# A first MLP product made of seven block products, with weight sums by adding DMAs, and GpSimd without arithmetic

## The chip, the core and the metric

The kernel runs on one core of one Trainium2 chip, in one launch. The metric is the time of one execution on the device in microseconds; shown is the median of several executions. The profile comes from one further execution.

## The reference, cut to what matters

One layer of a decoder, for 512 positions of width 1024, in float32:

```python
h = rms_norm(x, norm_mix)
proj = h @ w_in                      # HGRN2 and attention heads side by side
x = x + mixed @ w_out                # mixed: the heads' outputs
h = rms_norm(x, norm_xattn); mem_n = rms_norm(mem, norm_mem)
x = x + cross_attention(h, mem_n, w_xq, w_xk, w_xv, w_xo)
h = rms_norm(x, norm_mlp)
x = x + square(relu(h @ w_ff1)) @ w_ff2      # w_ff1 1024 x 4096, w_ff2 4096 x 1024
return rms_norm(x, norm_final)
```

`rms_norm` divides each position by the root of its mean square plus 1e-6 and multiplies by a gain.

## The kernel before

**Products.** Activations lie with features on the 128 partitions and positions in columns (T = 512). Each product is computed to nearly float32 accuracy by three matmuls: a weight `wr` is split into `wh` (rounded to fp32r, on ScalarE) and `wl = wr - wh` (VectorE), the activation likewise into `hi` and `lo`, and TensorE adds `wh*hi + wh*lo + wl*hi` in PSUM. A *unit* is a weight tile of 128x1024 (512 KB): one feature block of 128 outputs over all 1024 inputs, 8 blocks x 3 = 24 matmuls. `need(u)`, called ahead of unit u, issues the loads (up to six units ahead, three raw buffers, on SP's queue) and the splits (two units ahead, four buffers) of later units.

**Order.** Up to the output projection's neighbourhood the program is written under `manual_schedule`: each engine executes in the order in which the code emits; a small model (`Pace`) with due times decides in between when pieces of side work (norms, recurrence, attention: the generators) are emitted. From `ordered.__exit__` on (L508), the rest, among it both MLP products, is ordered by the compiler's automatic scheduler. Each engine runs its own instructions in order and waits by semaphores.

**The stages.** The head computes the first units `hf` while x is loaded (`split_x`, `square_x`): xhi on ScalarE, xlo on VectorE; the sum of squares is collected in Sx (GpSimd) and Sy (VectorE); `split_part(..., PO)` gives three lower parts of weights to GpSimd. `nr` is the matmul that sums the squares over partitions with ones, in a high and a low part (`nrh`, `nrl`). During the output projection `wo` the memory's norm is made (`mem_prep`): squares `msq` on ScalarE, folded by GpSimd to Sm, then nr. `hgrn_pre` has two multiplications on GpSimd for each head (ke, eb).

**The MLP.** The first product (tile `f`) has 32 units with 512-wide matmuls; `ev_ff1` takes max(.,0) times the norm's factor on VectorE (`fft`) and squares it on ScalarE into the tiles g. The second product is made of seven block products (Strassen-Winograd): g in four blocks (2 halves of features x 2 halves of positions), w_ff2 in four blocks; seven products of sums of blocks, each 8 units of 24 matmuls of 128x256, into the banks X, Y and Z (`PLAN`). Sums of activation blocks (`op_p6` and so on) are made on VectorE, and `make_op` splits them. Sums of weight blocks (u, four sets of eight) are made early in DRAM: a copy by SP's queue, then a DMA that adds, issued by GpSimd (`block_sums`); one of these transfers is emitted with each load from unit 16 on.

**The end.** `norm_part` and `final_half` normalise each half of the positions; the last half's multiplications (`xgf`) are shared by VectorE and GpSimd, and SP's queue writes the output.

Most engine calls go through a helper, so their line in the profile is L115; the tile's name tells them apart.

Of the kernel before, what the change touches and what calls it, by code (L numbers as in the profile page):

```python
# [15 lines left out]
P = 128  # L16
D = 1024
T = 512
# [14 lines left out]
FF2 = MLP + 32  # L33
# [89 lines left out]
def hybrid_layer(ctx: ExitStack, tc: tile.TileContext, xT, memT, ws, vecs, consts, rots, out):  # L123
# [14 lines left out]
    WBUFS, N8, N2, N2E = 4, 12, 14, 8  # L138
# [4 lines left out]
    def s2(dtype, name):  # L143
        return sp.tile([P, T], dtype, tag="s2", name=name, bufs=N2)

    def e2(dtype, name):
        return ep.tile([P, T], dtype, tag="e2", name=name, bufs=N2E)
# [10 lines left out]
    def mem_view(t):  # L158
# [3 lines left out]
    raws, his, los, late = {}, {}, {}, []  # L162
# [4 lines left out]
    F1 = [ws[MLP + 16 * (n // 8) + n % 8] for n in range(32)]  # L167


    B11, B12, B21, B22 = ([ws[MLP + 16 * (2 * i + c) + 8 + 4 * j + n] for c in range(2) for n in range(4)]  # L170
                          for i in range(2) for j in range(2))
    U1, U2, U3, U4 = ([dram.tile([P, D], F32, name=f"u{b}_{j}") for j in range(8)] for b in range(1, 5))
    sources = [ws[u] for u in range(MLP)] + [F1[j // 2 + 16 * (j % 2)] for j in range(32)]
    sources += B11 + U1 + U2 + B22 + U3 + B21 + U4

    def block_sums():

        for o1, i1, a1, o2, i2, a2 in ((U1, B11, B12, U3, B12, B22), (U2, U1, B22, None, None, None),
                                       (U4, U2, B21, None, None, None)):
            for j in range(8):  # L180
                yield nc.sync.dma_start(o1[j], i1[j])
                if o2:
                    yield nc.sync.dma_start(o2[j], i2[j])
            for j in range(8):
                yield nc.gpsimd.dma_start(o1[j], a1[j], accum_op=ALU.add, max_dma_last_dim=D)  # L185
                if o2:
                    yield nc.gpsimd.dma_start(o2[j], a2[j], accum_op=ALU.add, max_dma_last_dim=D)

    AFTER = mybir.DependencyInfo(mybir.DependencyClass.Sync, mybir.DependencyReason.DATA)
    marks = [None]  # L190

    sums_of_blocks = block_sums()

    def load_unit(parts=((0, D),)):
        u = state["load"]
        if u >= FF2 and u % 4 == 3:
            raws[u] = late[0].tile([P, D], F32, tag="rawl", name=f"wr{u}", bufs=1)
        else:
            raws[u] = wpool.tile([P, D], F32, tag="raw", name=f"wr{u}", bufs=RAWS)
# [3 lines left out]
        if u >= 16:  # L203
            dma = next(sums_of_blocks, None)
            if dma is not None:
                tc.add_manual_dep(dma.ins, marks[-2].ins.name, AFTER)

    def split_part(u, a, b, eng=None):
        A.activation(his[u][:, a:b], raws[u][:, a:b], AF.Copy)
        (eng or V).tensor_sub(los[u][:, a:b], raws[u][:, a:b], his[u][:, a:b].bitcast(F32))  # L210

    def split_begin():
        u = state["split"]
        his[u] = wpool.tile([P, D], F32R, tag="whi", name=f"wh{u}", bufs=WBUFS)
        los[u] = wpool.tile([P, D], F32R, tag="wlo", name=f"wl{u}", bufs=WBUFS)
        state["split"] += 1
        return u
# [5 lines left out]

    def need(u):
        marks.append(last_mm[0])
        want_load, want_split = min(UNITS, u + LOAD_AHEAD + 1), min(UNITS, u + SPLIT_AHEAD + 1)
        while state["split"] < want_split or state["load"] < want_load:
            if state["load"] < want_load and state["load"] - state["split"] < RAWS + (u >= FF2):
                load_unit()
            elif state["split"] < want_split:  # L230
                split_unit()
            else:
                break

# [169 lines left out]
    def square_x(k):  # L404
# [18 lines left out]
    split_part(0, 2 * P, D, PO)  # L423
# [3 lines left out]
    split_part(1, D // 2, D, PO)  # L427
# [4 lines left out]
    for k in range(4, KT):  # L432
        split_x(k)
        square_x(k - 2)
        if k == 6:
            split_unit(PO)
# [94 lines left out]
    def hgrn_pre(h):  # L531
# [6 lines left out]
        eb, enb = e2(F32, f"eb{h}"), e2(F32, f"kt{h}")  # L538
# [89 lines left out]
    def ev_q(h, acc):  # L628
        drain(("pre", h))
        H = head[h]  # L630
        qx = [sp.tile([P, 2, 224], F32, tag="s2", name=f"qx{g}", bufs=N2) for g in range(2)]
# [109 lines left out]
    def mem_prep():  # L741
# [12 lines left out]
        PO.tensor_add(sq[:, :1024], sq[:, :1024], sq[:, 1024:])  # L754
        PO.tensor_add(sq[:, :512], sq[:, :512], sq[:, 512:1024])
        PO.tensor_add(S[:, :M], sq[:, :M], sq[:, M:2 * M])
# [137 lines left out]
    def ev_xq(n, acc):  # L894
        z = s2(F32, f"xq{n}")
        V.scalar_tensor_tensor(z, acc, -float(M) ** -0.5, rb2, op0=ALU.mult, op1=ALU.mult)
        hi, lo = e2(F32R, f"xqh{n}"), e2(F32R, f"xql{n}")
# [23 lines left out]
    def ox_act(k):  # L921
# [3 lines left out]
    x2hi = [s8(F32R, f"x2hi{i}") for i in range(2)]  # L925
    x2lo = [s8(F32R, f"x2lo{i}") for i in range(2)]
    S2 = s2(F32, "S2")
    residual_stage(u, ox_act, "xo", [(2, 4)] + ONE * 6, lambda n: x1[n // 4][:, n % 4, :],
                   x1, G_MLP, x2hi, x2lo, S2)
    u += 8  # L930


    early.close()
    lp = ctx.enter_context(tc.tile_pool(name="late", bufs=1, reuse_waits="tile"))
    late.append(lp)
    rb3 = rb1
    start(norm_later(S2, rb3), "n3")
    x2_act = pair(x2hi, x2lo)
    half = T // 2
    g = [s8(F32, f"g{i}") for i in range(6)] + [lp.tile([P, 4, T], F32, name=f"g{i}") for i in (6, 7)]  # L940
# [5 lines left out]
    def ev_ff1(j, acc):  # L946
        n = j // 2 + 16 * (j % 2)
        if j == 0:
            drain("n3")
        t = s2(F32, "fft")  # L950
        V.scalar_tensor_tensor(t, acc, 0.0, rb3, op0=ALU.max, op1=ALU.mult)
        A.activation(g[n // 4][:, n % 4, :], t, AF.Square)
        if n >= 16 and n % 4 == 3:
            k = n // 4 - 4
            V.tensor_sub(part(k, 1), part(k + 4, 1), part(k, 1))

    fm_stage(u, x2_act, T, ev_ff1, "f1", [(2, 1)] + ONE * 30)
    u += 32
# [4 lines left out]
    def op_p1(k):  # L963
        return part(k, 0)

    def op_p5(k):
        return part(k, 1)

    def op_p6(k):
        V.scalar_tensor_tensor(part(k, 1), part(k, 1), -1.0, part(k, 0), op0=ALU.mult, op1=ALU.subtract)  # L970
        return part(k, 1)

    def op_p3(k):
        V.scalar_tensor_tensor(part(k, 0), part(k, 1), -1.0, part(k + 4, 0), op0=ALU.mult, op1=ALU.subtract)
        return part(k, 0)

    def op_p7(k):
        V.scalar_tensor_tensor(part(k, 1), part(k, 1), -1.0, part(k + 4, 1), op0=ALU.mult, op1=ALU.subtract)
        return part(k, 1)

    def op_p2(k):
        return part(k + 4, 0)

    def op_p4(k):
        return part(k + 4, 1)
# [3 lines left out]
    OPS = (op_p1, op_p5, op_p6, op_p3, op_p7, op_p2, op_p4)  # L989

    def make_op():

        i = op_state[0]
        op_state[0] += 1
        src = OPS[i // 4](i % 4)
        if i == 1:
            pieces = [[s2(F32R, f"op1{x}{y}") for x in range(2)] for y in range(2)]
        else:
            both = (lp.tile([P, 4, T], F32R, name="op0") if i == 0 else s8(F32R, f"op{i}")).rearrange("p a b -> p (a b)")
            pieces = [[both[:, :D], both[:, D:]]]  # L1000
# [31 lines left out]
    xg = {}  # L1032
    squares = [0, 0]

    def norm_part(h, t, n):
# [3 lines left out]
        if t not in xg:  # L1039
            xg[t] = mem_view(s8(F32, f"xgf{t}"))  # L1040
        q = Sf[t] if squares[t] == 0 else s2(F32, f"fsq{f}")
        A.activation(q[:, :half], d, AF.Square)
        A.activation(xg[t][:, f], d, AF.Copy, scale=gain(G_FIN, f))
# [3 lines left out]
        elif squares[t] == KT:  # L1047
            start(final_half(t, Sf[t], q, xg[t]), ("fin", t))

    def final_half(nb, S, q, xg):  # L1050
# [8 lines left out]
        for eng, a, b in ((V, 0, 2), (PO, 2, 4), (V, 4, 7), (PO, 7, 8)):  # L1059
            eng.tensor_mul(xg[:, a:b], xg[:, a:b], r[:, None, :].to_broadcast([P, b - a, half]))  # L1060
            SY.dma_start(out[nb, :, a:b], xg[:, a:b])
# [38 lines left out]
    drain(("fin", 1))  # L1100
    assert u + 56 == UNITS
# [73 lines left out]
```

## Time and profile before

| | us |
|---|---|
| median of 3 executions | 771.53 (771.48 to 773.09) |
| the profiled execution | 771.99 |
| its span in the profile | 770.2 |
| TensorE busy (4120 matmuls) | 746.6 |
| VectorE busy | 481.6 |
| ScalarE busy | 375.1 |
| GpSimd busy | 69.4 |
| first MLP product on TensorE, 768 matmuls | 418.4 to 592.6 |
| second MLP product | to 758 |

The span is what the profile covers, from the first to the last instruction; the execution's own time is 1.8 us longer. PE is TensorE's matmul, PEld its weight load, DVE VectorE, ACT ScalarE, POOL GpSimd, SP the engine that only issues DMAs. In a row of the trace the numbers are start and duration in us, and in brackets at the end the idle time of the engine just before the row and what ended it.

### The profile page before, as it was taken

To read this page: it belongs to the slowest core of one execution; us is meant where nothing else is said; L and a number is where in the kernel's file an instruction comes from. 1 tells how busy PE (TensorE), PEld (TensorE's weight loads), DVE (VectorE), ACT (ScalarE), POOL (GpSimd) and SP (SyncE) were. 2 spreads that over 40 slices of the span, in tenths; PEclk is the share of its full clock that TensorE was granted. 3 is DMA by queue.
4 is the path that set the end of the run, shared out by engine and by line. 5 is a ranking of instruction groups with operands and counts; after the bars stand their busy time and mean duration, and the time that the engine had idled before them with its cause. 6 is when DMAs were issued, how large, how long until landed. Compare 5 with 4: busy or idle time off the path is not lost.

```text
span 770.2 us, 10538 instructions
## 1 busy us (share of the span) xinstructions
PE 746.6 (97%) x4120; PEld 643.5 (84%) x4120; DVE 481.6 (63%) x747; ACT 375.1 (49%) x553; POOL 69.4 (9%) x67
## 2 busy tenths in 40 slices
PE   6999999999998999999999999999999999999993
PEld 4788888777786998888888888888888999999993
DVE  6889644877766655766466334243435898676862
ACT  7574546345755453555344433232325455476653
POOL 5123000000132210021001200000000000000011
PEclk9999999999999999999999999999999999999997
DMA  7413434544799997479668872323232555555531
GB/s 269 137 57 136 137 110 153 175 137 130 174 227 207 207 301 260 124 163 291 189 210 167 193 165 86 110 82 110 83 109 85 168 186 191 177 181 184 186 124 54
DMA packets 44801, 123.82 MB, mean 161 GB/s; under 512 B 4144, under 2 KB 21168, under 8 KB 44112
## 3 DMA queue, kind: packets, MB, share of 16 engines
q1 hardware_dynamic: 27376, 105.92, 40.4%
q0 software_dynamic: 16896, 16.78, 14.6%
q8 instruction: 32, 0.52, 0.3%
q10 hardware_dynamic: 480, 0.45, 0.2%
q14 instruction: 17, 0.14, 0.1%
HBM read 121.04 MB, written 35.65 MB: 203 GB/s over the span
## 4 chain that ended last, share of the span: by engine, by line
PE 88%; DVE 5%; issue 3%; ACT 2%; DMA 1%; POOL 0%; POOLq 0%; SPq 0%; DVEq 0%; ACTq 0%
PE f L115 22%; PE X L115 10%; PE xo L115 7%; PE Y L115 6%; PE mkq L115 6%; PE xq L115 6%; PE wo L115 5%; PE Z L115 3%; PE hq L115 3%; PE hg L115 3%; PE mv L115 3%; PE memv L115 3%; PE memk L115 3%; PE xs L115 1%; PE a L115 1%
## 5 line engine op out<-in xcount | busy, mean ns | idle before, releaser
L115 ACT ACTIVATE wh<-wr 128x1024 fp32r<-128x1024 f32 (+2 forms) x158 | 165.0, 1047 | 264.1 <-issue 113.3
L115 DVE TENSOR_TENSOR wl<-wr,wh 128x1024 fp32r<-128x1024 f32 (+1 forms) x155 | 188.7, 1219 | 57.0 <-ACT wh L115 56.4
L115 PE MATMUL f<-x2lo,wh 128*128 128x512 f32 x256 | 99.6, 389 | 0.0
L115 PE MATMUL f<-x2hi,wh 128*128 128x512 f32 x256 | 99.6, 389 | 0.0
L115 PE MATMUL f<-x2hi,wl 128*128 128x512 f32 x256 | 99.6, 389 | 0.0
L115 PE MATMUL X<-op,wh 128*128 128x256 f32 x512 | 93.6, 284 | 1.5 <-DVE op L115 0.8
L115 DVE SCALAR_TENSOR_TENSOR fft<-f,rb 128x512 f32<-128x512 f32 x32 | 22.0, 691 | 96.1 <-PE f L115 96.1
L115 PEld LDWEIGHTS X<-op,wh 128*128 128x128 f32 x512 | 80.1, 192 | 2.4 <-DVE op L115 1.3
L115 PE MATMUL X<-op,wl 128*128 128x256 f32 x256 | 72.4, 284 | 0.0
L115 PEld LDWEIGHTS f<-x2lo,wh 128*128 128x128 f32 x256 | 48.0, 188 | 10.1
L115 PEld LDWEIGHTS f<-x2hi,wl 128*128 128x128 f32 x256 | 48.1, 188 | 10.0
L115 PEld LDWEIGHTS f<-x2hi,wh 128*128 128x128 f32 x256 | 48.0, 188 | 10.0
L185 POOL DMA_DIRECT2D u<-in_ws_dram x24 | 24.5, 1022 | 316.0 <-DMA mraw<-in_memT_dram 129.4
L115 PEld LDWEIGHTS X<-op,wl 128*128 128x128 f32 x256 | 49.0, 192 | 0.1
L115 PE MATMUL Y<-op,wh 128*128 128x256 f32 x256 | 46.2, 283 | 0.0
L115 PEld LDWEIGHTS Y<-op,wh 128*128 128x128 f32 x256 | 39.9, 192 | 0.0
L115 DVE TENSOR_TENSOR op<-g,op 128x1024 fp32r<-128x1024 f32 (+1 forms) x29 | 34.0, 1183 | 5.1 <-ACT op L115 5.1
L115 PE MATMUL Y<-op,wl 128*128 128x256 f32 x128 | 36.2, 283 | 0.0
L115 POOL TENSOR_TENSOR xgf<-xgf,rb 128x512 f32<-128x512 f32 (+1 forms) x4 | 6.3, 1598 | 311.4 <-PE X L115 294.3
L115 ACT ACT_TABLE_LOAD x25 | 32.1, 1283 | 3.1 <-DVE osl L115 1.5
L115 ACT ACTIVATE op<-g 128x1024 fp32r<-128x1024 f32 (+1 forms) x29 | 29.0, 1019 | 4.2 <-PE X L115 1.5
L115 PE MATMUL mkq<-xhi,wl 128*128 128x512 f32 x64 | 26.6, 416 | 0.0
(268 smaller groups left out, 1625.4 us busy)
## 6 DMA issues: line engine op xcount, KB each, us to landing
wr<-in_ws_dram SPq DMA_DIRECT2D x122, 512.0 KB, 3.8
u<-in_ws_dram POOLq DMA_DIRECT2D x32, 512.0 KB, 6.7
wr<-u SPq DMA_DIRECT2D x32, 512.0 KB, 3.4
u<-in_ws_dram SPq DMA_DIRECT2D x16, 512.0 KB, 3.6
u<-u SPq DMA_DIRECT2D x16, 512.0 KB, 5.3
xraw<-in_xT_dram SPq DMA_DIRECT2D x8, 256.0 KB, 6.1
xr<-in_xT_dram SPq DMA_DIRECT2D x8, 256.0 KB, 6.5
mraw<-in_memT_dram SPq DMA_DIRECT2D x1, 1024.0 KB, 4.8
```

The costliest lines, as they stand in the source:

```text
L115: return f(*args, **kw)
L185: yield nc.gpsimd.dma_start(o1[j], a1[j], accum_op=ALU.add, max_dma_last_dim=D)
```

## The change

1. **The first product** is also made of seven block products. Its 32 units become 8 groups (`f1_group`), each for two output features blocks of each half of the 4096; w_ff1 is cut into E00, E01, E10, E11 (halves of the 1024 inputs x halves of the outputs... of a pair of blocks), so a group needs E00, E11, E10 and the sums B = E00 + E01, c = E11 + E01, A = B + E11, D' = E10 + A. Five raw loads per group go through SP's queue; `f1_load` adds E01 to B and to c by two DMAs of GpSimd's queue that add into SBUF; A and D' are VectorE additions (`f1_add`). Each product takes 2 banks x 4 blocks x 3 matmuls of 128x256; 56 splits of 128x1024 take the place of 32. Sums of the activation blocks (OA, OS, OB) are made in `ev_xo`, whose outputs come in the order 0, 4, 1, 5, 2, 6, 3, 7. The banks are taken out by copies (ScalarE) and additions (VectorE) into t1 and t2.
2. **GpSimd** computes nothing: its lower parts and sums in the head, ke and eb, the memory's squares and the last multiplications are VectorE instructions. It still issues the adding DMAs.
3. **The order**: both MLP products are under `manual_schedule`, so in written order. The ScalarE table with logarithm and exponential is loaded in groups 0 and 4 of the first product. Block sums of w_ff2 are emitted with the loads of units 16 to 67 (52) and in the first groups (12); their adding DMAs move pieces of up to 4096 instead of 1024 elements per descriptor row. The lower parts of weights have three buffers (four before) in the MLP; in the last block product the units come in the order 0, 2, 1, 3; the final norm's products are written into g tiles.

```diff
+    F1_ORDER = [(0, 1, 5, 3, 2, 4, 6)] * 7 + [(0, 1, 3, 2, 4, 5, 6)]
+    def f1_load(j, what):
+        r, c = {"A": (0, 0), "B": (0, 0), "C": (1, 1), "D": (1, 0)}[what.upper()]
+        t = f1raw[what, j] = raw_tile(f"w{what}{j}", what in "AD")
+        nc.sync.dma_start(two(t), E[r][c][j].rearrange("n p c -> p n c"))
+        if what in "Bc":
+            nc.gpsimd.dma_start(two(t), E[0][1][j].rearrange("n p c -> p n c"), accum_op=ALU.add)
+    def f1_add(j, out, x, y):
+        V.tensor_add(f1raw[out, j], f1raw[x, j], f1raw[y, j])
+    def f1_prep(j, s):
+        split_raw(split_begin(), f1raw[("ABCAcDd" if j == 7 else "ABDCAcD")[s], j], 0, D)
+        if s == 1:
+            f1_add(j, "A", "B", "C")
...
+        elif s == 1:
+            f1_load(j + 1, "B")
+        elif s == 3:
+            f1_add(j, "D", "D", "A")
+            f1_load(j + 1, "C")
...
+        if s in (2, 6):
+            more_sums()
...
     def need(u):
+        if MLP <= u + SPLIT_AHEAD < FF2:
+            f1_prep(*divmod(u + SPLIT_AHEAD - MLP, 7))
+            return
...
-    split_part(0, 2 * P, D, PO)
+    split_part(0, 2 * P, D, V)
...
-            S, eng = (Sx, PO) if k < 4 else (Sy, V)
+            S, eng = (Sx, V) if k < 4 else (Sy, V)
...
-        PO.tensor_add(sq[:, :1024], sq[:, :1024], sq[:, 1024:])
+        V.tensor_add(sq[:, :1024], sq[:, :1024], sq[:, 1024:])
...
-    fm_stage(u, x2_act, T, ev_ff1, "f1", [(2, 1)] + ONE * 30)
+    ordered = tc.manual_schedule()
+    ordered.__enter__()
+    for j in range(8):
+        f1_group(j)
+        u += 7
...
+            if p == 3 and j in (0, 4):
+                nc.scalar.preload_act_table_set("natural_log_exp_and_others")
...
+                for k in ks:
+                    a_hi, a_lo = op1(p, k)
+                    c = b * T + k * P
+                    w_hi, w_lo = his[w][:, c:c + P], los[w][:, c:c + P]
+                    mm(acc, w_hi, a_hi, p in (0, 1, 5) and k == 0, False)
+                    mm(acc, w_hi, a_lo, False, False)
+                    mm(acc, w_lo, a_hi, False, k == 3)
...
-        for eng, a, b in ((V, 0, 2), (PO, 2, 4), (V, 4, 7), (PO, 7, 8)):
+        for eng, a, b in ((V, 0, 2), (V, 2, 4), (V, 4, 7), (V, 7, 8)):
```

How the instructions stand on the engines, where the steps of the prediction speak of it. First VectorE in the first MLP product, before: a lower part (wl) for each unit, and one evacuation (fft) of each bank.

```order
L115 TENSOR_TENSOR wl_4555<-wr_4456,wh_4554 128x1024
L115 SCALAR_TENSOR_TENSOR fft<-f_4526,rb_217 128x512
L115 TENSOR_TENSOR wl_4589<-wr_4490,wh_4588 128x1024
L115 SCALAR_TENSOR_TENSOR fft<-f_4560,rb_217 128x512
L115 TENSOR_TENSOR wl_4624<-wr_4524,wh_4623 128x1024
L115 SCALAR_TENSOR_TENSOR fft<-f_4594,rb_217 128x512
```

The same engine now, in the third group (wl of c and D', taking out Y and X into t2, then wl of the next group's A and B, the sum A, and the factors):

```order
L115 TENSOR_TENSOR wl_4452<-wc_4210,wh_4451 128x1024
L115 TENSOR_TENSOR wl_4483<-wD_4241,wh_4482 128x1024
L115 TENSOR_TENSOR t_4399<-t_4399,Y_4385 128x256
L115 TENSOR_TENSOR t_4413<-t_4413,Y_4386 128x256
L115 TENSOR_TENSOR t_4399<-t_4399,X_4340 128x256
L115 TENSOR_TENSOR wl_4518<-wA_4419,wh_4517 128x1024
L115 TENSOR_TENSOR t_4413<-t_4413,X_4341 128x256
L115 TENSOR_TENSOR wl_4548<-wB_4307,wh_4547 128x1024
L115 TENSOR_TENSOR wA_4419<-wB_4307,wC_4383 128x1024
L115 SCALAR_TENSOR_TENSOR t_4399<-t_4399,rb_217 128x512
L115 SCALAR_TENSOR_TENSOR t_4413<-t_4413,rb_217 128x512
```

A lower part of the next group now stands between the two banks' evacuations of product 4, and a sum of weights ahead of the factors.

Second, TensorE in the output projection, before (wo_2053 is its fourth unit; the two nr are the memory's norm):

```order
L115 MATMUL wo_2053<-mixhi_1136,wl_1941 128x512
L115 MATMUL wo_2053<-mixhi_1693,wh_1940 128x512
L115 MATMUL wo_2053<-mixlo_1694,wh_1940 128x512
L115 MATMUL nr<-nrh,ones_r 128x256 [waits PE_49,Activation_49]
L115 MATMUL wo_2053<-mixhi_1693,wl_1941 128x512
L115 MATMUL wo_2053<-mixhi_1693,wh_1940 128x512
L115 MATMUL wo_2053<-mixlo_1694,wh_1940 128x512
L115 MATMUL nr<-nrl,ones_r 128x256 [waits DVE_49]
```

And now:

```order
L115 MATMUL wo_2055<-mixhi_1690,wl_1941 128x512
L115 MATMUL wo_2055<-mixhi_1690,wh_1940 128x512
L115 MATMUL nr<-nrh,ones_r 128x256 [waits PE_49,Activation_49]
L115 MATMUL wo_2055<-mixlo_1691,wh_1940 128x512
L115 MATMUL wo_2055<-mixhi_1690,wl_1941 128x512
L115 MATMUL nr<-nrl,ones_r 128x256 [waits DVE_49]
L115 MATMUL wo_2110<-mixhi_1121,wh_1998 128x512
```

The first nr stood behind 14 matmuls of that unit and now stands behind 22; the second stood behind 17 and now stands behind all 24.

Third, ScalarE at the end of the program, before:

```order
L115 ACTIVATE fsq_6754<-x_1905 128x256
L115 ACTIVATE xgf_6151<-x_1905,vec 128x256
L115 ACT_TABLE_LOAD
L115 ACTIVATE rb_2265<-fs,eps 128x256
L115 ACT_TABLE_LOAD
L115 ACTIVATE rb_2265<-rb_2265 128x256
```

And now:

```order
L115 ACTIVATE fsq_7624<-x_1898 128x256
L115 ACTIVATE g_3836<-x_1898,vec 128x256
L115 ACTIVATE fsq_7653<-x_1898 128x256
L115 ACTIVATE g_3836<-x_1898,vec 128x256
L115 ACTIVATE rb_2265<-fs,eps 128x256
L115 ACTIVATE rb_2265<-rb_2265 128x256
```

The two table loads ahead of the logarithm and the exponential are gone.

More of the change, by code (lines that the diff above doesn't have):

```diff
@@ L32 @@
 MLP = 8 + 8 + 4 + 8 + 4 + 4 + 4 + 4 + 8 + 8 + 8
-FF2 = MLP + 32
+FF2 = MLP + 7 * 8
 UNITS = FF2 + 7 * 8
@@ L159, in mem_view @@
         return t.rearrange("p a b -> p (a b)").rearrange("p (k m) -> p k m", k=KT)
-    raws, his, los, late = {}, {}, {}, []
+    raws, his, los, late, n8 = {}, {}, {}, [], [1]
     state = {"load": 0, "split": 0}
     LOAD_AHEAD, SPLIT_AHEAD, RAWS = 6, 2, 3
[L167 to L187, printed above, removed]
+    def f1_block(i, j):
+        us = [MLP + 16 * (n // 8) + n % 8 for n in range(16 * j, 16 * j + 16, 2)]
+        return [ws[u:u + 2, :, i * T:(i + 1) * T] for u in us]
@@ new lines, in f2_block, with two @@
+    def f2_block(i, j):
+        return [ws[MLP + 16 * (2 * i + c) + 8 + 4 * j + n] for c in range(2) for n in range(4)]
+    def two(ap):
+        return ap.rearrange("p (n c) -> p n c", n=2)
+    E, F = ([[f(i, j) for j in range(2)] for i in range(2)] for f in (f1_block, f2_block))
+    FU = [[dram.tile([P, D], F32, name=f"u{b}_{j}") for j in range(8)] for b in range(4)]
+    XO = (0, 4, 1, 5, 2, 6, 3, 7)
+    sources = [ws[u] for u in range(MLP - 8)] + [ws[MLP - 8 + n] for n in XO] + [None] * (FF2 - MLP)
@@ L189, in hybrid_layer, with more_sums, raw_tile @@
+    transfers = block_sums(F, FU)
+    SUMS_FROM = 16
     AFTER = mybir.DependencyInfo(mybir.DependencyClass.Sync, mybir.DependencyReason.DATA)
     marks = [None]
-    sums_of_blocks = block_sums()
+    def more_sums():
+        dma = next(transfers, None)
+        if dma is not None:
+            tc.add_manual_dep(dma.ins, marks[-2].ins.name, AFTER)
+    def raw_tile(name, in_late):
+        if in_late:
+            return late[0].tile([P, D], F32, tag="rawl", name=name, bufs=2)
+        return wpool.tile([P, D], F32, tag="raw", name=name, bufs=RAWS)
@@ L194, in load_unit @@
     def load_unit(parts=((0, D),)):
         u = state["load"]
[L196 to L199, printed above, removed]
+        raws[u] = raw_tile(f"wr{u}", u >= FF2 and (u - FF2) % 5 in (1, 3))
         for a, b in parts:
@@ L202, in load_unit, with later, split_raw, lower @@
         state["load"] += 1
[L203 to L206, printed above, removed]
+        if SUMS_FROM <= u < MLP:
+            more_sums()
+    held = []
+    def later(f):
+        held[0].append(f) if held else f()
+    def split_raw(u, raw, a, b, eng=None):
+        A.activation(his[u][:, a:b], raw[:, a:b], AF.Copy)
+        def lower(hi=his[u], lo=los[u]):
+            (eng or V).tensor_sub(lo[:, a:b], raw[:, a:b], hi[:, a:b].bitcast(F32))
+        later(lower)
     def split_part(u, a, b, eng=None):
-        A.activation(his[u][:, a:b], raws[u][:, a:b], AF.Copy)
-        (eng or V).tensor_sub(los[u][:, a:b], raws[u][:, a:b], his[u][:, a:b].bitcast(F32))
+        split_raw(u, raws[u], a, b, eng)
     def split_begin():
@@ L233, in need @@
                 break
+        if MLP - 6 <= u < MLP - 2:
+            for what in ("A", "B", "CD", "c")[u - MLP + 6]:
+                f1_load(0, what)
     side = []
@@ L630, in ev_q @@
         H = head[h]
-        qx = [sp.tile([P, 2, 224], F32, tag="s2", name=f"qx{g}", bufs=N2) for g in range(2)]
+        qx = [s2(F32, f"qx{g}", (2, 224)) for g in range(2)]
         rbeb = H["rbeb"].rearrange("p (t c) -> p t c", c=P)
@@ L936, in hybrid_layer, with op1 @@
+    fm_stage(u, ox_act, T, ev_xo, "xo", [(2, 4)] + ONE * 6)
+    u += 8
+    def op1(p, k):
+        if p == 0:
+            return OA[0][:, k, :half], OA[0][:, k, half:]
+        if p < 5:
+            return tuple(x[:, (p - 1) * half:p * half] for x in OS[k])
+        return tuple(x[:, (p - 5) * half:(p - 4) * half] for x in OB[k])
+    lp = late[0]
     rb3 = rb1
     start(norm_later(S2, rb3), "n3")
-    x2_act = pair(x2hi, x2lo)
-    half = T // 2
-    g = [s8(F32, f"g{i}") for i in range(6)] + [lp.tile([P, 4, T], F32, name=f"g{i}") for i in (6, 7)]
+    g = [s8(F32, f"g{i}") for i in range(8)]
@@ L958, in hybrid_layer @@
[L958 to L985, printed above, removed]
+    rest = []
+    def f1_tile(t, op, dst):
+        V.scalar_tensor_tensor(t, t, 0.0, rb3, op0=op, op1=ALU.mult)
+        A.activation(dst, t, AF.Square)
+    def f1_end(n, t):
+        k = n // 4
+        A.activation(g[k][:, n % 4, :], t, AF.Square)
+        if n % 4 == 3:
+            V.tensor_sub(part(k, 1), part(k + 4, 1), part(k, 1))
+    def f1_rest():
+        while rest:
+            rest.pop(0)()
```

247 lines of the change are left out of this document (191 added, 56 removed).

## The prediction

> **What bounds the kernel now.** I read the page first: the span, the busy time of each engine, and the shares of the chain that ended last. Then I read that chain in order of time, and then the two MLP stretches, 418.40 to 593.20 (first product) and 593.20 to 758.00 (second).
>
> ```profile
> span 770.2 us, 10538 instructions
> PE 746.6 (97%) x4120; PEld 643.5 (84%) x4120; DVE 481.6 (63%) x747; ACT 375.1 (49%) x553; POOL 69.4 (9%) x67
> PE 88%; DVE 5%; issue 3%; ACT 2%; DMA 1%; POOL 0%; POOLq 0%; SPq 0%; DVEq 0%; ACTq 0%
> ```
>
> TensorE is busy 97% of the span and holds 88% of the chain. Time can only go where matmuls become fewer or shorter, or in the 770.2 - 746.6 = 23.6 us in which TensorE stands. VectorE has 288.6 us left over, GpSimd computes little. The next rows are the chain (start, duration, engine, tile, count) and then windows (start:end, length, and the busy time of PE, PEld, DVE, ACT, POOL with counts, granted clock, DMA share, GB/s; the last of the three counts tile f alone, on PE, PEld, DVE).
>
> ```profile
> 426.55 163.94 PE f L115 x723
> 617.97 23.04 PE Y L115 x192
> 418.40:593.20 174.80, 174.80 (x772) 144.68 (x771) 69.25 (x73) 58.70 (x73) 6.10 (x6) 1.00 0.42 118
> 593.20:758.00 164.80, 163.34 (x1351) 162.39 (x1350) 124.23 (x123) 94.71 (x114) 3.16 (x2) 1.00 0.50 163
> 418.40:593.20 174.80, 174.23 (x768) 144.14 (x768) 21.36 (x31) 1.00 0.42 118
> ```
>
> In the first product TensorE never stands: 163.94 / 723 = 226.7 ns from one 512-wide matmul to the next. The second product, already made of block products, runs its 256-wide matmuls at 23.04 / 192 = 120.0 ns, with VectorE busy 124.23 / 164.80 = 75% beside it and only 1.46 us of TensorE idle. The clock granted is 1.00 in both.
>
> **Step 1, the first product.** It removes 768 matmuls of 128x512 and adds 8 groups x 7 products x 2 banks x 4 blocks x 3 = 1344 of 128x256. By the paces above: 768 x 226.7 = 174.1 us go, 1344 x 120.0 = 161.3 us come, **-12.8 us**. The ideal is 7/8 (-21.8); a 256-wide matmul costs 120.0 and not 113.4, and that takes 9 us back. The pace of 120.0 holds as bound from below; from above it can only grow by waits, which the rivals price.
>
> By the Trainium skill, "TensorE: Matmul & The Clock Gate", section "Back-to-back issue gap", an isolated matmul takes N/2.4 + 2.5 ns, so 109.2 and 215.8: by that the step would give 165.7 - 146.8 = -19 us, an estimate. Both measured paces lie about 11 ns above it, so the trace does not agree, and the rows are kept.
>
> Whether the other engines keep up I take from these groups (count | busy us, mean ns | idle before):
>
> ```profile
> L115 DVE TENSOR_TENSOR wl<-wr,wh 128x1024 fp32r<-128x1024 f32 x153 | 187.6, 1228 | 56.4 <-ACT wh L115 55.8
> L115 ACT ACTIVATE wh<-wr 128x1024 fp32r<-128x1024 f32 x154 | 162.5, 1058 | 263.1 <-issue 113.3 <-PE X L115 30.7 <-PE f L115 21.9
> L115 DVE SCALAR_TENSOR_TENSOR fft<-f,rb 128x512 f32<-128x512 f32 x32 | 22.0, 691 | 96.1 <-PE f L115 96.1
> L115 DVE TENSOR_TENSOR x<-x,X 128x256 f32<-128x256 f32 x4 | 1.7, 422 | 6.1 <-PE X L115 6.1
> L115 ACT ACTIVATE g<-fft 128x512 f32<-128x512 f32 x32 | 19.6, 615 | 0.0
> ```
>
> A group is 168 x 0.120 = 20.16 us on TensorE. VectorE gets per group 7 lower parts and 2 sums of weights, 9 x 1.228, ten 256-wide evacuations x 0.422 (taken from the 256-wide addition out of a bank), two 512-wide x 0.691, and every second time a block difference of about 1.2: 11.05 + 4.22 + 1.38 + 0.6 = 17.2 us, 86%. ScalarE gets 7 x 1.058 + 6 copies of 256 (0.42 as on VectorE) + 4 squares x 0.615 = 12.4 us. Both fit, so the work is hidden, at a cost of nothing if no single wait is late. A product is 24 x 0.120 = 2.88 us; a lower part is made two products ahead (5.76 us) and a raw bank's evacuation has at least the other bank's 1.44 us. A row-by-row walk in written order gave no wait, the smallest margins being about 0.9 us (the second bank of product 4, behind one 1.2 us lower part) and 0.1 us at the start, where the norm's row sum must be broadcast in the first group. Bounds: 0 and, if each of the eight groups loses one such lower part, 8 x 1.2 = +10. I take 0, for the second product runs at 75% with 1.46 us idle, and keep +10 for the range.
>
> Its transfers: five loads and two adding DMAs of 512 KB per group, plus two of the block sums in six groups.
>
> ```profile
> q0 software_dynamic: 6773, 6.73, 62.9%
> q1 hardware_dynamic: 4744, 17.30, 28.7%
> wr<-in_ws_dram SPq DMA_DIRECT2D x122, 512.0 KB, 3.8
> u<-in_ws_dram POOLq DMA_DIRECT2D x32, 512.0 KB, 6.7
> L185 POOL DMA_DIRECT2D u<-in_ws_dram x24: 1005/1014/1201, 198.2 to 447.3; - x24
> DMA to landing us min/median/max: 3.1/4.3/23.4
> ```
>
> The first row is the adding queue between 212 and 283 us (packets, MB, share of 16 engines): 0.629 x 71 / (6.73 / 0.524) = 3.5 us of all engines for one add. The second is the loads between 418 and 593: 0.287 x 175 / 33 = 1.5 us each. A group asks 5 x 1.5 + 2 x 3.5 = 14.5 us of 20.16, with two more transfers of the block sums up to 21.5 for six groups. Those rows are of adds into DRAM in 1 KB pieces; the new ones go into SBUF in 2 KB pieces, and the block sums in 4 KB, for which no row exists. Lower bound as a plain load, 7 x 1.5 = 10.5, upper 14.5 to 21.5. I take the hidden case, since with fewer packets the true price should lie on the load's side of the middle, and since block sums can arrive late with no reader near: the load of a sum comes a block product later.
>
> **Step 2, GpSimd's arithmetic goes to VectorE.** In the head, one GpSimd operation beside a VectorE one slows both:
>
> ```profile
> 18.22 2.43 DVE L115 SCALAR_TENSOR_TENSOR xlo<-xraw,vec,xhi 128x512 fp32r<-128x512 f32 x2
> L115 DVE TENSOR_TENSOR xsq<-xraw 128x512 f32<-128x512 f32 x4 | 7.1, 1781 | 0.0
> 20.06 2.84 POOL L115 TENSOR_TENSOR wl<-wr,wh 128x1024 fp32r<-128x1024 f32 x1
> 22.95 0.50 PE L115 MATMUL hf<-xhi,wl 128*128 128x512 f32 x1 [0.36 <-POOL wl L115]
> 27.81 0.49 PE L115 MATMUL nr<-nrh,ones_r 128*128 128x512 f32 x1 [0.24 <-ACT nrh L115]
> 28.89 0.50 PE L115 MATMUL nr<-nrl,ones_r 128*128 128x512 f32 x1 [0.58 <-DVE nrl L115]
> 29.22 0.40 PE L115 MATMUL hf<-xhi,wh 128*128 128x512 f32 x1
> ```
>
> A square takes 1.78 us on the mean here, against 0.69 for the 512-wide operation above that runs alone. VectorE gains 768 + 512 + 1024 elements of lower parts (about 2.7 us) and three sums (2.0), and loses the four slowed squares' excess (about 4 x 1.1) and what xlo loses (a pair 2.43 against 1.4, twice). Walked in the new order, the last xlo ends near 19.5 instead of 20.65 (-1.1), the wait for wl goes (-0.36), the norm's sums are ready near 23.3, so that nr finds them there (-0.24 - 0.58), and some 0.2 of smaller gaps: the fourth unit starts near 26.7, not 29.22, **-2.5 us**. Bounds 0 (VectorE's added 4.7 us cancel all) and -3.0.
>
> Before the memory's norm, GpSimd adds the squares in 5.2 us, and the broadcast waits twice:
>
> ```profile
> 226.62 4.10 POOL L115 TENSOR_TENSOR msq<-msq 128x1024 f32<-128x1024 f32 x2 [2.25 <-ACT msq L115]
> 231.34 1.08 POOL L115 TENSOR_TENSOR Sm<-msq 128x256 f32<-128x256 f32 x1
> 233.51 0.39 PE L115 MATMUL nr<-nrh,ones_r 128*128 128x256 f32 x1 [1.82 <-ACT nrh L115]
> 235.17 0.39 PE L115 MATMUL nr<-nrl,ones_r 128*128 128x256 f32 x1 [0.58 <-DVE nrl L115]
> ```
>
> On VectorE the three adds take 1.2 + 0.7 + 0.4 = 2.3 us between other rows, and the first nr stands behind 21 to 22 matmuls of that unit instead of 14: 7 x 0.227 = 1.6 us later. 1.82 + 0.58 go, **-2.4 us** (bounds 0 and -2.4).
>
> **Step 3, the written order and the end.** The second product's first operand parts now come in the last group:
>
> ```profile
> 597.50 0.38 PE L115 MATMUL X<-op,wh 128*128 128x256 f32 x1 [0.81 <-DVE op L115]
> PE X L115 <- DVE x L115: 0.6, 1, 0.6
> ```
>
> Both waits go, **-1.4 us**; bounds -1.5 and +1 (lower part of the last unit 1.5 us before its reader, by the walk). The end:
>
> ```profile
> 759.02 0.70 PE L115 MATMUL fs<-fsq,ones 128*128 128x256 f32 x2 [0.53 <-ACT fsq L115]
> 759.39 1.28 ACT L115 ACT_TABLE_LOAD   x1
> 760.68 0.47 ACT L115 ACTIVATE rb<-fs,eps 128x256 f32<-128x256 f32 x1
> 761.17 1.28 ACT L115 ACT_TABLE_LOAD   x1
> 762.47 0.42 ACT L115 ACTIVATE rb<-rb 128x256 f32<-128x256 f32 x1
> 762.92 2.63 DVE L115 TENSOR_TENSOR xgf<-xgf,rb 128x512 f32<-128x512 f32 x2 [4.40 <-ACT rb L115]
> 762.96 3.16 POOL L115 TENSOR_TENSOR xgf<-xgf,rb 128x512 f32<-128x512 f32 x2 [17.14 <-ACT rb L115]
> ```
>
> The changed order has no table load after the last one in group 4. The first load begins at 759.39, before the matmul's end near 759.7, so 0.3 of it was hidden: 2.56 - 0.3 = 2.2 us go. Two engines took from 762.89 to 766.12 for 2048 columns, 3.23 us; VectorE alone needs 4 x 0.69 = 2.76, so the last multiply ends 0.5 us sooner after rb: **-2.7 us** (bounds -2 and -3.5). The output's last DMA behind it is the same.
>
> **Sum.** -12.8 - 2.5 - 2.4 - 1.4 - 2.7 = -21.8: span 770.2 to 748.4. The profiled execution took 771.99, 1.8 more than its span, and lies 0.46 over the median of 771.53. That gives 750.2 for such a run and 749.7 for a median; I say **750**.
>
> **The rivals.** (a) *VectorE or ScalarE late by order.* At 86% a row that waits for a bank holds up the lower part behind it. For it: 0.1 us margin at the start and 17.2 of 20.16 us. Against: 75% goes with 1.46 us in the second product. One lower part per group, 8 x 1.2 = 10: about 760, from 754 up.
>
> (b) *The DMA engines full.* If adds into SBUF cost 3.5 us and the block sums as much, six groups want 21.5 of 20.16 us, 1.3 x 6 = 8 us, and loads for D with only 6.7 us of lead land late behind adds, 1 to 2 us more each group: 758 to 775.
>
> (c) *Slower.* The place is B = E00 + E01, whose plain load is issued a group (20.16 us) before its split; less 3.3 us to land and 1.0 to issue, the add has 15.9 us. If it lands later, ScalarE stands at wB, VectorE behind it, and TensorE. Each microsecond beyond costs 8, so 21.8 / 8 = 2.7: from 18.6 us on it is slower. At 23.4 us, the largest landing of any transfer into u, whichever queue, it costs 8 x 7.5 = 60, less 22: about 810. The median landing of 6.7 speaks against it, as does the issue row (1005 to 1201 ns through all of VectorE's work); for it, that all adds share one queue, whose head can wait for a buffer.
>
> The Trainium skill, "SBUF — State Buffer", section "Who interferes with whom", says that a DMA issued by GpSimd can starve for descriptors while VectorE runs in a two-port mode, which speaks against adding DMAs beside an 86% VectorE. The trace has no sign of it in the issue row; the landings of wB will tell.
>
> (d) *No gain from 256-wide matmuls.* Break-even is at 174.1 / 1344 = 129.5 ns. At 130 step 1 gives +0.6, the other steps -9.0: 763.6. Against it stands the row of 120.0, of the same shape and weight loads.
>
> The skill's section on the issue gap also gives sustained paces: 131 ns for N = 512 and 81 for N = 128. By these 768 x 131 = 100.6 us would become at least 1344 x 81 = 108.9, a loss of 8 us or more on the step, an estimate; the trace's 226.7 ns does not agree with the first of them.
>
> (e) *Exactly half.* If a 256-wide matmul beside a less busy weight path took half of 226.7, 113.4 ns, step 1 gives -21.8: 741. The 120.0 row, with 1351 matmuls in 163.34 us around it (120.9), speaks against it.
>
> **How the numbers follow.** The main case, 746.5 to 754, has 0.65 (its lower end is the sum of the favourable bounds, 771.5 - 23.2, less 2 us of idle TensorE time that I did not place), (a) 754 to 763 0.18; (b) 0.10; (c) 0.05; (d) 0.01, (e) 0.01. The time is the main case's, 750. The range of 746.5 to 762 leaves out (c), (e) and the upper parts of (a) and (b), under 2 in 10. Within 0.2% (1.5 us, about what a measurement can tell) ends only a piece of (b): 0.02. Slower: (c) and a rest of (b), 0.05. Faster: 0.93.
>
> **What would show it.** Right: 1344 matmuls of the blocks in 161 to 163 us, TensorE idle in that stretch under 2 us; the fourth unit at 26.7; no wait at the memory's nr; no table load after the last matmul, and the end 8 to 9 us after it, not 12. Wrong: a row of idle time before those matmuls whose releaser is DVE wl or DVE t (a), a DMA share near 1.0 there (b), wB as releaser of ScalarE with landings over 16 us (c), a pace near 130 ns (d).

## The result and the profile after

Two statements ahead of the prediction need setting right. Only the head, up to L508, is under `manual_schedule` in the kernel before; the output projection is not. And the first index of E00, E01, E10, E11 is the half of the 1024 inputs, the second the half of the outputs.

The changed kernel takes 759.25 us (median of 4, 756.95 to 760.02), the kernel before, beside it, 771.50. The ratio is 0.9832, 95% interval 0.9807 to 0.9857: 12 us faster. Forecast were 750 and 746.5 to 762. The sign and the range held; the time lies outside the main case of 746.5 to 754, the size of the gain was a little over half of what I said, and the runs spread over 3 us where those of before agree within 2.

The profiled execution is the fastest of the four (756.95, span 755.2). Its page:

```profile
span 755.2 us, 11996 instructions
PE 735.1 (97%) x4696; PEld 664.0 (88%) x4696; DVE 545.5 (72%) x891; ACT 415.5 (55%) x634; POOL 49.4 (7%) x62
PE 87%; DMA 4%; ACT 3%; DVE 3%; issue 2%; SPq 0%; DVEq 0%; ACTq 0%
```

DMA, 1% of the chain before, is now 4%. The chain in order of time says which transfers these are, and how fast the first product's matmuls run (start, duration, what):

```profile
446.42 11.52 PE X L115 x96
...
484.00 7.33 DMA wA<-in_ws_dram
505.24 9.27 DMA wA<-in_ws_dram
528.40 8.34 DMA wA<-in_ws_dram
```

These three are plain loads of E00 for the next group, landing after 7.3 to 9.3 us. The pace of the first product's matmuls, where none waits, is as forecast, 11.52 / 96 = 120.0 ns. The stretches (columns as before; first product, second product):

```profile
413.50:582.90 169.40, 164.47 (x1347) 163.47 (x1346) 131.21 (x178) 95.48 (x145) 24.32 (x22) 0.99 0.79 207
582.90:746.00 163.10, 162.54 (x1351) 162.23 (x1350) 126.85 (x127) 92.65 (x114) 0.00 (x0) 1.00 0.51 168
```

The first product takes 169.4 us instead of 174.65 (418.65 to 593.3 before), and TensorE idles 4.9 us in it. The rest of the 15.0 us of span came from elsewhere: 5.15 before the first product, 1.6 in the second, 2.9 behind it.

TensorE's idle time there (last bracket: idle us and who ended it), and one such wait followed back over VectorE, ScalarE, SP's queue and GpSimd's queue:

```profile
494.11 0.39 PE L115 MATMUL X<-OBh,wh 128*128 128x256 f32 x1 [0.17 <-DVE t L115]
517.28 0.39 PE L115 MATMUL X<-OBh,wh 128*128 128x256 f32 x1 [2.75 <-DVE t L115]
539.52 0.39 PE L115 MATMUL X<-OBh,wh 128*128 128x256 f32 x1 [1.82 <-DVE t L115]
...
511.69 0.42 DVE L115 TENSOR_TENSOR t<-t,X 128x256 f32<-128x256 f32 x1 [0.60 <-PE X L115]
515.67 1.23 DVE L115 TENSOR_TENSOR wl<-wA,wh 128x1024 fp32r<-128x1024 f32 x1 [3.56 <-ACT wh L115]
516.82 0.41 DVE L115 TENSOR_TENSOR t<-t,X 128x256 f32<-128x256 f32 x1
...
514.58 1.06 ACT L115 ACTIVATE wh<-wA 128x1024 fp32r<-128x1024 f32 x1 [3.95 <-DMA wA<-in_ws_dram]
...
505.24 0.37 SPq L281 DMA_DIRECT2D wA<-in_ws_dram  x1
...
501.51 1.23 POOL L283 DMA_DIRECT2D wB<-in_ws_dram  x1 [3.59 <-DMA wB<-in_ws_dram]
502.24 1.41 POOL L200 DMA_DIRECT2D u<-in_ws_dram  x1
```

Read from below: two adding DMAs, B's and a block sum's, are issued 0.7 us apart at 501.5 and 502.2; the load of A follows at 505.24 and lands 9.3 us later; ScalarE stands 3.95 us for it, VectorE 3.56; and the second bank of product 4 (t at 516.82), which had been ready at about 514.5, is taken out only behind that lower part, so product 6 can't begin.

### The profile page after: what moved, and what is told of

Read it like the earlier page. It is cut to its first block, busy times and chain, and to the rows that moved or that the text cites. A ratio compares the mean times of both kernels' runs of the same rounds, so it can differ in the third digit from the quotient of the medians.

```text
span 755.2 us, 11996 instructions
## 1 busy us (share of the span) xinstructions
PE 735.1 (97%) x4696; PEld 664.0 (88%) x4696; DVE 545.5 (72%) x891; ACT 415.5 (55%) x634; POOL 49.4 (7%) x62
## 4 chain that ended last, share of the span: by engine, by line
PE 87%; DMA 4%; ACT 3%; DVE 3%; issue 2%; SPq 0%; DVEq 0%; ACTq 0%
PE X L115 19%; PE Y L115 12%; PE xo L115 7%; PE mkq L115 6%; PE xq L115 6%; PE wo L115 5%; DMA wA<-in_ws_dram 3%; PE hf L115 3%; PE Z L115 3%; PE hg L115 3%; PE mv L115 3%; PE memv L115 3%; PE hq L115 3%; PE hi L115 3%; PE memk L115 2%
## 5 line engine op out<-in xcount | busy, mean ns | idle before, releaser
L115 ACT ACTIVATE wh<-wr 128x1024 fp32r<-128x1024 f32 (+2 forms) x126 | 130.4, 1041 | 121.2 <-PE wo L115 19.6
L115 DVE TENSOR_TENSOR wl<-wr,wh 128x1024 fp32r<-128x1024 f32 (+2 forms) x126 | 151.5, 1205 | 40.7 <-ACT wh L115 26.4
L115 PE MATMUL Y<-OS,wh 128*128 128x256 f32 x256 | 47.2, 284 | 0.2 <-ACT t L115 0.2
L115 PE MATMUL X<-OS,wh 128*128 128x256 f32 x256 | 46.5, 283 | 0.0
L115 PEld LDWEIGHTS Y<-OS,wh 128*128 128x128 f32 x256 | 39.9, 192 | 0.5 <-ACT t L115 0.4
L115 PEld LDWEIGHTS X<-OS,wh 128*128 128x128 f32 x256 | 39.9, 192 | 0.0
L115 PE MATMUL X<-OS,wl 128*128 128x256 f32 x128 | 36.2, 283 | 0.0
L115 PE MATMUL Y<-OS,wl 128*128 128x256 f32 x128 | 36.2, 283 | 0.0
L115 ACT ACTIVATE op<-g 128x1024 fp32r<-128x1024 f32 x28 | 29.2, 1045 | 0.5 <-PE X L115 0.5
L115 DVE TENSOR_TENSOR op<-g,op 128x1024 fp32r<-128x1024 f32 x24 | 29.3, 1219 | 0.0
```

The lines of the kernel that those rows point to most:

```text
L115: return f(*args, **kw)
```

## The experiments

**Theory T:** the DMA engines are full while block sums run in the groups, A lands late, and the order on VectorE hands this to TensorE. **Rival V:** VectorE, at about 80% there, has too much to do. All times below are medians of four runs, each series beside runs of the kernel before at 772.1 to 772.5; the ratio to these stands with its interval.

**Taking the bank out first.** Only the place of one lower part moves:

```diff
-                if p == 4 and b == 0:
+                if p == 4 and b == 1:
                     for lower in held.pop():
                         lower()
```

> Only VectorE's order in the first MLP product changes: in product 4 of each group the second bank is taken out before the lower part of the next group's A, not after it. Theory T (a late load of A holds VectorE, and the second bank's evacuation stands behind it, so TensorE waits): the waits of product 6 for t (2.75 + 1.82 + 0.17 us) go, and with them most of the slow matmuls behind them; time 752 to 755 against 757 to 760 of the changed kernel. A still lands late, so that some 0 to 1 us may appear at the next group's first product. Theory V (VectorE at 86% has too much to do, whatever its order): the waits move to other rows, time 757 to 760.

Measured 756.81 us (755.18 to 760.10; 0.9802, 0.9775 to 0.9829), within the changed kernel's own spread: a miss for T's number. The waits of product 6 for t are gone, but A still lands late (6.6 us on the median, at most 9.5), and waits appear where A itself is read, and once for a bank's copy by ScalarE in the last group:

```profile
516.38 1.06 ACT L115 ACTIVATE wh<-wA 128x1024 fp32r<-128x1024 f32 x1 [5.31 <-DMA wA<-in_ws_dram]
...
517.49 0.51 PE L115 MATMUL X<-OA,wh 128*128 128x256 f32 x2 [1.09 <-ACT wh L115]
518.75 0.39 PE L115 MATMUL X<-OA,wl 128*128 128x256 f32 x1 [0.76 <-DVE wl L115]
...
568.00 0.50 PE L115 MATMUL Y<-OS,wh 128*128 128x256 f32 x2 [1.67 <-ACT t L115]
```

So while A is late, VectorE's order chooses the place of the wait. The last row is a price of the new order itself: 0.90 us of it stays when A comes in time (the run with both cures, below).

**The last 12 block-sum transfers with the second product's loads:**

```diff
-        if SUMS_FROM <= u < MLP:
+        if SUMS_FROM <= u < MLP or u >= FF2:
             more_sums()
...
-        if s in (2, 6):
-            more_sums()
```

> The 12 transfers of block sums that run in the first product's groups are emitted with the loads of the second product instead; VectorE's order is that of the changed kernel. Theory T with the DMA engines as the cause of the late load: the DMA share in groups 2 to 6 falls from 0.79 to 0.95 to about 0.6 to 0.75, A lands in 4 us instead of 6.5 to 9.3, and the waits for t are under 0.5 us together; time 750 to 753. If instead the adding DMAs into SBUF alone make A late, A lands as late as before and the time stays at 757 to 760. Theory V: no change, 757 to 760.

Measured 751.51 us (751.08 to 751.64; 0.9726, 0.9710 to 0.9743). The first product's window:

```profile
413.70:576.10 162.40, 162.22 (x1348) 161.85 (x1347) 130.96 (x179) 95.03 (x145) 19.37 (x17) 1.00 0.71 190
```

162.4 us, against 161.3 in the prediction's first step, with 0.18 us of idle time, VectorE just as busy (131.0 against 131.2 us) and A landing in 4.5 us on the median. V falls; the 7.7 us between this kernel and the changed one are what moving the block sums' transfers out of the groups is worth. In the two profiles the first product is 7.0 us shorter, and the second 1.5 longer, where these transfers now run.

**No addition into B and c** (another sum is computed):

```diff
-        if what in "Bc":
+        if False and what in "Bc":
             nc.gpsimd.dma_start(two(t), E[0][1][j].rearrange("n p c -> p n c"), accum_op=ALU.add)
```

> Leaves out the two adding DMAs of each group (B is E00 alone and c is E11 alone, so this computes other sums); everything else as in the changed kernel, block sums included. Theory T: without 16 adds the DMA share in the groups falls by 2 x 3 us of 20.16, so to about 0.6, A lands in 4 us, no wait for t; time 750 to 753. By how much the share falls gives the price of one add into SBUF: 3.5 us of all engines by the rows of the adds into DRAM, 1.5 if it costs no more than a load. Theory V: 757 to 760.

Measured 750.06 us (0.9709, 0.9695 to 0.9724), no wait for t. Taking away either kind of adding DMA cures it. The price of one add comes from the queue rows (packets, MB, share of 16 engines) between 454 and 555 us: of the kernel with the later sums, in which this queue only adds into SBUF, and then of this one, in which it only adds into DRAM.

```profile
q0 software_dynamic: 2787, 5.38, 33.3%
```

```profile
q0 software_dynamic: 1152, 4.19, 24.7%
```

0.333 x 101 / (5.38 / 0.524) = 3.3 us of all engines for 512 KB into SBUF in 2 KB pieces, and 0.247 x 101 / (4.19 / 0.524) = 3.1 into DRAM in 4 KB pieces. Larger pieces made an add hardly cheaper than the 3.5 us of the 1 KB pieces before.

**More transfers, fewer of them adds ahead of A.** `SUMS_FROM` is 20 in place of 16, so that 16 transfers (eight copies, then eight adds) fall to the groups.

> The opposite dose: 16 transfers of block sums in the first product's groups in place of 12 (two in every group), the head's share smaller by four. Theory T (DMA engines full): waits also in groups 7 and 8, 1 to 2.5 us each, time 760 to 764, DMA share over the stretch 0.82 to 0.85. If the amount of transfers does not matter: 757 to 760.

Measured 755.54 us (754.54 to 756.52; 0.9781, 0.9765 to 0.9798), faster than the changed kernel instead of slower: T as put here, by the amount of transfers, is wrong. Both kernels have eight block-sum adds in the groups (of the changed kernel's 12 transfers the first four are copies); here four more copies come first, and the adds later. Between 454.0 and 494.3 us this kernel has only copies beside its loads and B's and c's adds, and after 500 us the adds; the last row is the first stretch in the changed kernel, which has three block-sum adds there:

```profile
454.00:494.30 40.30, 40.30 (x338) 40.30 (x338) 32.25 (x44) 21.98 (x34) 4.82 (x4) 1.00 0.84 237
500.00:575.00 75.00, 71.57 (x580) 70.96 (x579) 54.83 (x72) 40.88 (x62) 14.10 (x14) 0.98 0.88 215
```

```profile
454.00:494.30 40.30, 40.12 (x334) 39.92 (x334) 31.08 (x43) 22.20 (x34) 6.36 (x6) 1.00 0.87 217
```

A DMA share of 0.84 with copies cost TensorE nothing; 0.88 with adds cost 3.4 us. The share does not decide by itself: the changed kernel's first adds, at 0.87, cost only 0.18 us in this stretch, and its waits come in the groups behind. The landings say more: here A landed in 4.5 and 5.5 us in the two groups between 454 and 494 us, with copies, and in 7.5, 5.9 and 8.8 in the three behind, with adds; in the changed kernel, with adds, in 6.0 and 7.3 and then 9.3 and 8.3. So the late landings of A go with the adding transfers. Whether their number or their place in the group makes them late, this run doesn't show.

**The same 12 transfers, placed elsewhere in the group,** so that none stands directly behind B's add:

```diff
-        if s in (2, 6):
+        if s == 0:
+            more_sums()
             more_sums()
```

> The changed kernel with the same 12 block-sum transfers in the same six groups, but both of a group emitted at its first split, so behind the addition into c and ahead of the load of B; none stands directly behind the addition into B any more. Theory P (the damage is done by the pair of adding DMAs 0.7 us apart, 3 to 4 us ahead of the load of A): A lands in 3.3 to 6 us, the waits of product 6 for t go, 751 to 753.5, at an unchanged DMA share of 0.79 to 0.83. Theory T as first put (the amount of transfers fills the engines, wherever they stand): A or another load is late all the same, 757 to 760.

Measured 756.52 us (755.30 to 757.96; 0.9803, 0.9787 to 0.9820), between the two theories and nearer to T. A lands in 5.2 us on the median, but two loads of B take 10.4 us. Behind one of them the sum B is late, and TensorE waits 3.9 us in the product, 2.4 of it still for t:

```profile
539.24 1.06 ACT L115 ACTIVATE wh<-wB 128x1024 fp32r<-128x1024 f32 x1 [4.06 <-DMA wB<-in_ws_dram]
```

Against the changed kernel the other place brings 2.7 us between the medians, with intervals that overlap; having none of these transfers in the groups brings 7.7. Two adds now run back to back behind c's, so another place might do better. Why adds hurt more than copies at a like share stays open: no run gave the loads an engine or queue of their own.

**Both cures at once,** the later block sums and the bank taken out first:

> The later block sums and, besides, product 4's second bank taken out ahead of the lower part of the next A. If VectorE's order costs only where A is late, nothing is left to gain: 751.5 as with the later sums alone. If the order costs by itself: 749 to 750.5.

Measured 753.03 us (752.86 to 753.33; 0.9751, 0.9737 to 0.9766): 1.5 slower than the later sums alone, where nothing was expected. In the profile TensorE waits 0.90 us once for a bank's copy in the last group, and 0.6 and 0.8 us for lower parts at the second product's start; the order as changed was the better one once A came in time.

**GpSimd's arithmetic.** All of it back, in the changed kernel (`V` to `PO` at the ten calls); then the head's, and the memory's additions, alone, from the kernel with the later sums.

> The changed kernel with all arithmetic of GpSimd given back to it (head, ke and eb, memory squares, last multiplications): what remains is the first product by blocks and the written order. By the steps: head +2.5 to +3.5, memory norm +1.5 to +2.4, last multiplications +0.5, so 4.5 to 6.5 us slower than the changed kernel, 762 to 766. If the arithmetic's place does not matter: 757 to 760.

> From the kernel with the later block sums (751.5): the head's three lower parts and the sums into Sx go back to GpSimd, alone. By step 2 of the prediction 2.5 us slower, with the hf to hq waits 2.5 to 3.7: 754.0 to 755.3, with xsq and xlo at 1.2 to 2.9 us again. The rival, that VectorE carries these instructions at the same price and the head is bound by the loads of x: 751.5.

> From the kernel with the later block sums (751.5): the memory's three additions go back to GpSimd, alone. If they cost what the prediction's row said, the waits of nr come back (1.8 + 0.4 to 0.6) and the new wait of nc (1.07) goes: net 1.0 to 1.5 us slower, 752.5 to 753.0; if TensorE's clock is granted at half for some 3 us behind that wait, as in the kernel with all of GpSimd's arithmetic, 1.3 more, so about 754. If the place of these additions does not matter: 751.5.

Measured 766.46 us (762.75 to 767.23; 0.9912, 0.9886 to 0.9939) for all, 7.2 over the changed kernel; 755.95 for the head (0.9788, 0.9774 to 0.9803), 4.4 over the later sums; 753.93 for the memory (752.57 to 754.98; 0.9761, 0.9740 to 0.9782), 2.4 over. For all of it, 2.6 us of the difference between the profiles lie in the first product, which has no GpSimd arithmetic: its waits for t are 3.61 and 2.06 us there, with the half clock of the last section behind both. In the head's profile the first product begins 3.1 us later (416.8 against 413.7), which is step 2's own size, another 0.8 lie in the second product, and the slowing of VectorE beside GpSimd is back:

```profile
L115 DVE SCALAR_TENSOR_TENSOR xlo<-xraw,vec,xhi 128x512 fp32r<-128x512 f32 x8 | 8.9, 1139 | 6.4 <-ACT xhi L115 6.4
L115 DVE TENSOR_TENSOR xsq<-xraw 128x512 f32<-128x512 f32 x4 | 7.1, 1778 | 0.0
```

The changed kernel's rows for xlo and for the squares:

```profile
L115 DVE SCALAR_TENSOR_TENSOR xlo<-xraw,vec,xhi 128x512 fp32r<-128x512 f32 x8 | 6.0, 749 | 6.3 <-ACT xhi L115 6.3
...
L115 DVE TENSOR_TENSOR xsq<-xraw x4: 684/685/687, 12.6 to 21.8; 128x512 f32<-128x512 f32 x4
```

The memory's additions alone moved the first product by 0.7 us (414.4 against 413.7). The stretch from the start of hi to that of memk grew by 1.1 us: nr waits 2.22 us again, and nc's 1.10 goes. Another 0.9 lie in the second product, where the edit changes nothing, and the clock stayed at 1.00 behind the wait.

**Without the two preloads of ScalarE's table,** from the kernel with the later sums:

```diff
-            if p == 3 and j in (0, 4):
-                nc.scalar.preload_act_table_set("natural_log_exp_and_others")
```

> From the kernel with the later block sums (751.5): the two preloads of ScalarE's table in groups 0 and 4 are left out, alone. Then the last norm loads two tables behind the last matmul: 2.2 us at the end by the prediction's step, so 753.7; a table load in the first group may add up to 0.5. If the loads there are hidden: 751.5.

Measured 756.27 us (755.55 to 757.03; 0.9790, 0.9775 to 0.9805), 4.8 slower and not 2.2. At the end it is the expected 2.1 (from the last product matmul's start to the span's end 11.6 against 9.5 us). The other half lies earlier: 1.2 in the first group, where a bank's copy now stands behind the norm's table loads, and 1.1 in the second product, with 0.66 for a lower part late in it:

```profile
430.24 0.50 PE L115 MATMUL X<-OS,wh 128*128 128x256 f32 x2 [1.09 <-ACT t L115]
...
731.44 0.39 PE L115 MATMUL X<-op,wl 128*128 128x256 f32 x1 [0.66 <-DVE wl L115]
```

**Two more steps in the direction of the runs.** One load of the table that holds both functions, held behind a matmul ahead of the memory's norm; then also the 12 transfers at every third load of the second product (`u >= FF2 and u % 3 == 0`).

```diff
         yield [S[:, :M]]
+        t = nc.scalar.preload_act_table_set("natural_log_exp_and_others")
+        tc.add_manual_dep(t.ins, last_mm[0].ins.name, AFTER)
         yield from norm_rows(S, M, rbm, rcm)
```

> From the kernel with the later block sums (751.5): one load of the table that serves both the logarithm and the exponential, placed ahead of the memory's norm, in place of the two loads within it. The wait of nc for rbm (1.07 us, 1.24 with the restart) should go: 750.3. If nc then waits for something else, or the load holds up a split: 751 to 752.

> The kernel with the memory's one table load (750.6), and the 12 block-sum transfers at every third load of the second product instead of every load. The three waits of Y for wl there (0.18 + 0.69 + 0.69 us), where twelve transfers run together, should go: 749.0 to 749.8. If they are not due to those transfers: 750.6.

Measured 750.63 us (0.9719, 0.9704 to 0.9733) and 748.80 us (748.68 to 749.16; 0.9697, 0.9682 to 0.9711). The wait for rbm went, and with the spread the three waits for wl at the second product's start. The last one is the fastest kernel of the study: 10.4 us under the changed one and 23.5 under the one before.

## Why the prediction was right and wrong

The range held because it takes in the rivals' times: 759.25 is close to rival (a)'s "about 760", but by another cause, and that is luck.

**Step 1, -12.8, became -5.25.** The paces were right: with the later block sums the stretch is 162.4 us. Of the 8.1 us over the forecast 161.3, 4.9 are waits, put at nothing in the sum, and about 1.4 the half clock behind one of them. What failed is the sum's sentence on the transfers, "I take the hidden case, since with fewer packets the true price should lie on the load's side of the middle". An add into SBUF measured 3.3 us and one into DRAM with four times longer pieces 3.1, both near the row's 3.5 and not near a load's 1.5. The sum counted two more adds in each of six groups; only eight of the twelve transfers are adds, so it is four groups. In these, with 14 us for their own loads and adds and some 6 for two adds of block sums, the demand is about the 20 us that a group has, an estimate close to the upper bound that I had written down. Rival (b), at 0.10, comes nearest to what happened, at its lower edge (758): adds as dear as it said, and loads that land late behind them. But the load was A's and not D's, and the DMA share that I had named as its sign was not near 1.0: it was 0.79 in the product and 0.86 between 454 and 555 us, and the run with 16 transfers shows that the amount alone doesn't decide.

Rival (a) had the right place (the second bank of product 4 behind a lower part), and its sign, DVE t as the releaser, came; but it had the wrong cause: that order costs nothing when A lands in time. Rival (c) did not come: an add into B landed in 7.0 us on the median and one into c in 5.7, against the 15.9 it had. The Trainium skill's warning in "SBUF — State Buffer", section "Who interferes with whom", that a DMA issued by GpSimd can starve while VectorE runs in a two-port mode, shows no trace here: the adds' issue took 1.20 to 1.25 us beside VectorE at 78%. No row says whether VectorE ran in that mode. (d) and (e) are out by the 120.0 ns.

**Step 2, the head, -2.5, became -2.9**, and another 0.8 came that I had not listed: TensorE's wait of 0.63 us for Vh ahead of hq is gone. Undone alone it costs 3.1 us up to the first product. The two nr no longer wait:

```profile
25.87 0.40 PE L115 MATMUL nr<-nrh,ones_r 128*128 128x512 f32 x1
26.11 0.40 PE L115 MATMUL nr<-nrl,ones_r 128*128 128x512 f32 x1
```

**Step 2, the memory, -2.4, became about -1.45,** of which the run that undoes it alone shows 1.1. The waits of nr went, as said, and what was late next I had not named: the transposition of the norm, nc, now stands closer behind, and waits while ScalarE loads two tables for it.

```profile
229.72 0.38 PE L115 MATMUL nr<-nrh,ones_r 128*128 128x256 f32 x1
230.41 0.28 PE L115 MATMUL nr<-nrl,ones_r 128*128 128x256 f32 x1
235.66 0.61 PE L115 MATMUL nc<-ident,rbm 128*128 128x1 f32 x4 [1.07 <-ACT rbm L115]
```

**Step 3.** The second product lost 1.6 us (forecast 1.4). The end became 2.9 us shorter (forecast 2.7): no table load stands there, and the last multiplications take 2.50 us on VectorE.

```profile
746.98 0.70 PE L115 MATMUL fs<-fsq,ones 128*128 128x256 f32 x2 [0.53 <-ACT fsq L115]
747.71 0.47 ACT L115 ACTIVATE rb<-fs,eps 128x256 f32<-128x256 f32 x1 [0.39 <-PE fs L115]
748.22 0.42 ACT L115 ACTIVATE rb<-rb 128x256 f32<-128x256 f32 x1
748.67 2.50 DVE L115 TENSOR_TENSOR g<-g,rb 128x512 f32<-128x512 f32 x4 [2.19 <-ACT rb L115]
```

The sum: -2.9 - 0.8 - 1.45 - 5.25 - 1.6 - 2.9 = -14.9, the span's 15.0 but for rounding. It is made against the profiled execution, 2.3 us under the median; how the waits for A vary from one execution to the next was not followed further.

## What to carry to other kernels

Price the transfers of a stretch like an engine: add up what it asks of the DMA engines per period, and if the dear end of an unknown price fills the period, give that rival more than a tenth. The sum alone is not enough: ask which load would land late, and who reads it next. An adding DMA cost about twice a load here, with pieces of 1, 2 and 4 KB alike; background adds did least harm in the stretch with DMA time left, and spread out. When a wait is taken away, look for the next reader on the same chain (here nc behind nr).

## What was not expected of the hardware

TensorE's granted clock fell to about half for 3 to 4 us behind some short waits, and not behind others. In the changed kernel, after the waits that end at 539.52 (1.82 us) and at 517.28 (2.75 us):

```profile
539.50:543.50 4.00, 3.98 (x21) 3.98 (x22) 4.00 (x6) 1.13 (x2) 1.76 (x2) 0.58 0.57 96
517.20:521.20 4.00, 3.92 (x32) 3.92 (x33) 4.00 (x7) 1.06 (x2) 1.35 (x2) 1.00 0.78 120
```

21 matmuls in 4 us instead of 32: a wait of 1.82 us cost about 1.4 more. The granted clock was 0.57 in the 4 us behind waits of 1.92 us (the run with 16 transfers), 2.06 and 3.61 us (the run with GpSimd's arithmetic back), and 1.00 behind waits of 1.67 us (the bank taken out first) and 1.75 us (the transfers placed elsewhere). In the kernel with GpSimd's arithmetic back it came behind the memory's two nr, 1.81 and 0.37 us:

```profile
235.80:239.00 3.20, 3.20 (x8) 2.62 (x9) 0.00 (x0) 0.48 (x1) 0.00 (x0) 0.50 0.89 330
```

The kernel before had the same two waits (1.82 and 0.58 us) and kept its clock of 1.00. The Trainium skill, "TensorE: Matmul & The Clock Gate", section "What's actually happening", says that the clock halves after an idle window of about 3.4 us and rises after as much busy time; the half clock and its length agree with that, but it came here after waits of about half that length, and a longer one (2.75 us) had none behind it. No run tells what decides.
